# The first 128 tokens of x for three head groups by VectorE's 32x32 turning and a trip through DRAM, in place of TensorE's transposes

## The chip, the core and the metric

The kernel runs on one core of one Trainium2 chip. The metric is the device time of one execution in microseconds (us). A core has five engines that each work through a list of instructions of their own, in order: TensorE (PE, the matrix products; its weight loads are shown as PEld), VectorE (DVE), ScalarE (ACT), GpSimd (POOL) and SyncE (SP). DMA transfers are issued by SP, ACT or POOL and carried out by 16 DMA engines. SBUF is the memory on the core, 128 partitions wide; PSUM is the small memory into which TensorE writes.

## The reference, cut to what matters

One inference step of a one-layer decoder with a gated MLP half and a state-space (SSD) half, for 256 prompt tokens and 8 samples of 8 tokens. What the change touches is the SSD half:

```python
xbc, new_conv = causal_depthwise_conv(xbc, conv_state, conv_w, conv_b)
xbc = jax.nn.silu(xbc)
xs = xbc[..., :SSM_WIDTH].reshape(bsz, L, SSM_HEADS, SSM_HEAD_DIM).astype(f32)   # 32 heads of 64
dt = jax.nn.softplus(dt_raw.astype(f32) + dt_bias.astype(f32))
...
xdt = (x * dt[..., None]).reshape(bsz, nc, q, G, R, P)          # 4 groups of 8 heads, chunks of 128 tokens
cb = jnp.einsum("bctgn,bcsgn->bctsg", cc, bc)
y_diag = jnp.einsum("bctsgr,bcsgrp->bctgrp", cb[..., None] * decay, xdt)
states = jnp.einsum("bcsgn,bcsgr,bcsgrp->bcgrpn", bc, decay_states, xdt)
```

The product `xdt` is needed with tokens on the partitions, since both `y_diag` and `states` sum over tokens; the convolution that makes `xs` leaves channels on the partitions. So x has to be turned. The prompt is two chunks of 128 tokens (c = 0 and c = 1); the 64 sample tokens are a third piece.

## The kernel before

All 320 tokens stand side by side in the free dimension and channels on the partitions. The large products go through `project` (columns of `w_in` and `ffn_w_up`) and `chunk_out` (rows of `w_out` and `ffn_w_down`). Each loads weights slab by slab (`slab`, line 109: 512 KB on SP's queue into three buffers in turn, a rounded copy `whi` made by ACT on line 123, the remainder `wlo` by DVE on line 124) and runs three products per block on TensorE (lines 134 to 136).

The SSD half works through four groups of 8 heads, each a generator `ssd(g)` (line 901). Its steps are put between the large products: after every slab `tick` (line 157) advances the first task in the list when enough products have gone by (`yield 24, 0` means 24 products later). Four generators stand one behind the other. The x of group g + 1 is made by `heads_in_next(g + 1)` (line 1209) while group g is under way: `conv_proj` projects, convolves, and its last activation (lines 459 and 460, on ACT) writes block j of `xs`.

At the beginning of a group (lines 959 to 965), for each chunk c, TensorE turns four blocks of 128 channels by 128 tokens of `xs` with `by_token` (line 410) into a PSUM tile `xt_ps`, and `times` (line 923) multiplies it with `dt` into `xdt[:, c]` on DVE. From chunk 0 POOL makes the decayed copy `x0d` (`decayed(0, 0)`, line 930), ACT and DVE split it into `x0s` (lines 981 and 982, a tile with the tag `xsp`), and 48 products later TensorE multiplies it with B into `s_ps` (line 991). Then come the steps n = 0 to 12 (line 1106), 24 products apart. At steps 2, 5, 7 and 10 `end(i)` updates two sample states each (products `up_ps`, line 1018, which read the tile `xsp` of the samples); at steps 6 and 12 `products` makes y (`y_ps`, line 1086); at step 11 `mask_c` prepares the next group's C mask on DVE. `tc.issue_after(lowered[0])` puts DVE instructions behind the last `wlo` that the code has issued at that point. The tag `xsp` has one buffer: `x0s`, then `xsp`, then the next group's `x0s` take it in turn, each after the last reader of the one before.

A way to turn by DVE and DRAM is there already for B: `to_tokens` (line 414) turns 32x32 blocks of 64 tokens on DVE into a tile with the tag `pv` (four buffers), and POOL writes them to `b_d` in DRAM with four DMAs per 64 tokens; they are loaded again with tokens on partitions (`b_raw`, line 839). Within a row the channels then stand as (i j f), i the 32-row block, j the block of 128, f within 32, and `in_order` (line 423) reads them in their order.

The build derives the waits between engines from the tiles that instructions read and write, and lays out each engine's list from the order in the code, priorities (`first()`, `tc.high_priority`), the `issue_after` edges, and when it estimates operands to be ready; so instructions of one engine need not run in the order of the code.

Of the kernel before, what the change touches and what calls it, by code (L numbers as in the profile page):

```python
# [8 lines left out]
F32 = mybir.dt.float32  # L9
# [3 lines left out]
ALU = mybir.AluOpType  # L13
# [3 lines left out]
P = 128  # L17
NP = 256
NB, TS = 8, 8
NS = NB * TS  # L20
NT = NP + NS
# [12 lines left out]
def hybrid_step(  # L34
# [10 lines left out]
    act, dve, pool, pe, sp = nc.scalar, nc.vector, nc.gpsimd, nc.tensor, nc.sync  # L45
# [4 lines left out]
    dr = ctx.enter_context(tc.tile_pool(name="dr", bufs=1, space=DRAM))  # L50
    wp = ctx.enter_context(tc.tile_pool(name="wp", bufs=3))
    tp = ctx.enter_context(tc.tile_pool(name="tp", bufs=2))
# [3 lines left out]
    def misc(name):  # L56
        return ms.tile([P, 512], F32, tag="ms", name=name)
# [6 lines left out]
    with tc.high_priority(offset=300000):  # L64
        dve.memset(ones, 1.0)

        ps = misc("early")
# [39 lines left out]
    slab_load, split_after, both, rounded, lowered = [], [None], [], [], []  # L107
# [248 lines left out]
    tot_d = dr.tile([NH, NB], F32, name="tot_d")  # L356
    s1_d, x1_d = ([dr.tile([P, 512], F32, name=f"{n}_d{g}") for g in range(3)] for n in ("s1", "x1"))
    b_d = dr.tile([NT, 512], F32, name="b_d")
    v_d = [dr.tile([NT, 2 * P], F32, name=f"v_d{i}") for i in range(KD // 2)]
    ssq_d = [dr.tile([P, NT // 32], F32, name=f"ssq_d{i}") for i in range(4)]  # L360

# [48 lines left out]
    def by_token(ps, x, c):  # L410

        pe.transpose(ps, x[:, P * c:P * c + P], ident)  # L412

    def to_tokens(x, rows):

        for o in range(0, NT, NS):
            t = tp.tile([P, NT], F32, tag="pv", name="turned", bufs=4)[:, :4 * NS].rearrange("p (r f) -> p r f", r=2)
            dve.transpose(out=t.rearrange("p r (j f) -> p r j f", j=4), in_=x[:, :, o:o + NS].rearrange("p j (r t) -> p r j t", t=32))
            for i in range(4):
                pool.dma_start(rows[o:o + NS, P * i:P * i + P].rearrange("(r t) f -> t r f", t=32), t[32 * i:32 * i + 32])  # L420
            yield

    def in_order(ap):
# [3 lines left out]
    with ExitStack() as mctx:  # L427
        op = mctx.enter_context(tc.tile_pool(name="op", bufs=1))
# [42 lines left out]
        dt = op.tile([P, 5, NH], F32, name="dt")  # L471
# [115 lines left out]
        with tc.tile_pool(name="gp", bufs=1) as gp:  # L587
# [42 lines left out]
            def root():  # L630

                dve.tensor_tensor(out=acc[:, 0, :], in0=acc[:, 0, :], in1=acc[:, 1, :], op=ALU.add)
                ps = misc("tsum")
                for c in range(2):
                    pe.matmul(ps[:, c:c + 1], acc[:, 0, P * c:P * c + P], ones[:, 0:1], start=True, stop=True)
                for h in range(2):
                    pe.matmul(ps[64 * h:64 * h + 64, 2:3], acc[:, 0, NP:NT], ones[:, 0:1], start=True, stop=True, tile_position=(0, 64 * h))
                return rsqrt_of(ps[:, 0:3], 1.0 / D, 3)
# [42 lines left out]
            ps = [mm.tile([P, 512], F32, tag="mm", name=f"ps_v{j}") for j in range(4)] + [misc(f"ps_v{j}") for j in (4, 5)]  # L681
            for kt in range(KD):
                x_ready(kt, 1)
                x = [h[:, kt, :] for h in hT]
# [24 lines left out]
                if kt == 15:  # L709
                    r = root()  # L710
# [6 lines left out]
            turned = [gp.tile([P, 4, NT], F32, tag="vf", name="turned", bufs=2).rearrange("p j n -> p (j n)") for _ in range(2)]  # L717
            turned = [t[:, 2 * NT * h:2 * NT * h + 2 * NT].rearrange("p (s j f) -> p s j f", j=2, f=32) for t in turned for h in range(2)]
# [121 lines left out]
            for g in range(4):  # L840
# [3 lines left out]
                if g < 3:  # L844
                    uf = gate_up(g + 1)
                    if g == 2:
                        b4 = [[tp.tile([P, NT], F32, tag="pv", name="b4", bufs=4)[:, :256] for _ in range(2)] for _ in range(2)]
                        for i in range(2):
                            o = NP + 32 * i
# [8 lines left out]
        with tc.tile_pool(name="sd", bufs=1) as sd:  # L858
# [36 lines left out]
            def by_head(ap):  # L895
                return ap.rearrange("p (h d) -> p h d", d=64)

            x_of = {0: x0}
            rest, y_made, b_later = [], {}, []

            def ssd(g):

                xs = x_of[g]
                h0 = 8 * g
# [17 lines left out]
                xdt = sd.tile([P, 3, 512], F32, tag="xdt", name="xdt", bufs=1)  # L922
                def times(out, ps, c, at=slice(0, P), h=slice(0, 8)):
                    n = h.stop - h.start
                    dve.tensor_tensor(out=by_head(out), in0=by_head(ps),
                                      in1=dt[at, c, h0 + h.start:h0 + h.stop].unsqueeze(2).to_broadcast([at.stop - at.start, n, 64]), op=ALU.mult)

                def decayed(i, c):
                    xde = sd.tile([P, 512], F32, tag="xde", name="xde", bufs=2)
                    pool.tensor_tensor(out=by_head(xde), in0=by_head(xdt[:, c, :]),  # L930
                                       in1=dec[:, i, h0:h0 + 8].unsqueeze(2).to_broadcast([P, 8, 64]), op=ALU.mult)
                    return xde
# [20 lines left out]
                def samples_rows(ps):  # L953
                    for r in range(2):
                        at, hs = slice(NS - NS * r, P - NS * r), slice(256 * r, 256 * r + 256)
                        dve.tensor_tensor(out=by_head(xdt[at, 2, hs]), in0=by_head(ps[:NS, hs]),
                                          in1=dt[:NS, 2, h0 + 4 * r:h0 + 4 * r + 4].unsqueeze(2).to_broadcast([NS, 4, 64]), op=ALU.mult)

                for c in range(2):
                    ps = misc("xt_ps")  # L960
                    for j in range(4):
                        by_token(ps[:, P * j:P * j + P], xs[:, j], c)
                    times(xdt[:, c, :], ps, c)
                    if c == 0:
                        x0d = decayed(0, 0)
                ps = misc("cb_ps")
# [3 lines left out]
                for r in range(2):  # L970
# [3 lines left out]
                                  in0=ps[:, :NP].rearrange("p (c t) -> p c t", c=2),  # L974
                                  in1=upper.unsqueeze(1).to_broadcast([P, 2, P]), op=ALU.mult)
# [51 lines left out]
                def yo_to_xdt():  # L1027

                    for r in range(2):
                        at = slice(64 * r, 64 * r + 64)  # L1030
                        dve.tensor_tensor(out=by_head(xdt[at, 2, 256 * r:256 * r + 256]), in0=by_head(ps_yo[at, :256]),
                                          in1=ed[at, g, :].unsqueeze(2).to_broadcast([64, 4, 64]), op=ALU.mult)
# [10 lines left out]
                xsp = sd.tile([P, 2, 512], F32R, tag="xsp", name="xsp", bufs=1)  # L1043
# [62 lines left out]
                for n in range(13 - e):  # L1106
                    if n == 0:
                        samples_rows(ps_x)
                        yo_to_xdt()
                    if n in ends and not (n == 10 and g == 3):  # L1110
                        end(ends[n])
                    for i in picks.get(n, ()):
                        bms[i] = picked(i)
                    if n in (6, 12 - e):
                        products(0 if n == 6 else 2)
                        products(1 if n == 6 else 3)
                    with tc.issue_after(last_made[0]):
                        for j in decays_of.get(n, ()):
                            cs_of[j] = load_sums(j)
                        if n == 8 and g < 3:  # L1120
                            first_sums[g + 1] = load_sums(0, g + 1, h0 + 8)
                        if n in states and states[n][0] < 4:
                            sts_of[states[n][0]].append(load_state(*states[n]))
                    if n == 9 and g == 3:
                        b_raw = sd.tile([P, 512], F32, tag="st", name="b_later", bufs=6)
                        sp.dma_start(b_raw, b_d[P:2 * P])
                        b_later.append(b_raw)
                    if n == 11 and g < 3:
                        with tc.issue_after(lowered[0]):
                            mask_c(g + 1)  # L1130
                    if n in shrinks:
                        shrunk(shrinks[n], sts[shrinks[n]])
                    if n in heads:
                        with tc.issue_after(last_made[0]):
                            decays(heads[n])
                    if n < 12 - e:
                        yield 24, 48 if n + 1 in (0, 1, 2, 5, 7, 10) and (g < 3 or n < 7) else 0
# [3 lines left out]
                                   in1=dec[:, 2, h0:h0 + 8].unsqueeze(2).to_broadcast([P, 8, 64]), op=ALU.mult)  # L1141
# [98 lines left out]
            with first():  # L1240
# [4 lines left out]
                with tc.issue_after(sums_ins[-1]):  # L1245
                    ps = token_sums(*one)
# [3 lines left out]
                r = rsqrt_by_root(most, ps, 1.0 / D)  # L1250
# [54 lines left out]
    with tc.tile_pool(name="fp", bufs=1) as fp:  # L1305
# [118 lines left out]
        ps = misc("tsum")  # L1424
# [7 lines left out]
        v, s, r, t = (fp.tile([P, SN], F32, name=f"last_{i}") for i in "vsrt")  # L1432
# [7 lines left out]
        f, x = (t.rearrange("p s k f -> p s (k f)") for t in (f_tok, x1_tok))  # L1440
# [121 lines left out]
```

## Time and profile before

| | |
|---|---|
| median of 3 runs | 1748.12 us (1747.77 to 1748.39) |
| the profiled execution | 1747.88 us |
| its span, first to last instruction | 1746.1 us |
| granted TensorE clock | 0.999 |
| DMA moved | 303.85 MB, mean 174 GB/s |
| first and last turning of prompt x on TensorE | 419.2 and 670.0 us |

The span is the time between the first and the last instruction in the trace; what the profiled execution took beyond it (1.8 us) lies around it. In a row of the timeline the columns are start, length, engine, line, operation, output and inputs; in square brackets stands idle time of the engine before it and who ended it. The chain of waits is followed back from the last instruction, at each step to what released it or to the instruction before it on its engine; its pieces don't overlap, whereas TensorE's own records do, since products are pipelined. "Landing" is the time from the issue of a DMA to its end.

### The profile page before, as it was taken

Reading aid. Unit: us, or ns where it says so; the run is one execution under the profiler, and the core shown is the slowest. Engines: PE = TensorE matmul, PEld = TensorE weight load, DVE = VectorE, ACT = ScalarE, POOL = GpSimd, SP = SyncE. Lnnn points to the kernel's source line nnn. Section 1 sums busy time; section 2 is a strip of 40 time slices with the busy share of each in tenths; the row PEclk is TensorE's granted clock in tenths of the full one; section 3 lists DMA queues with packets and bytes.
Section 4 is the critical chain, followed back from the end, with each engine's and each line's share of the span. In section 5 each row is a group of like instructions: output and inputs, shape, how many; then the busy total and the mean of one; then the engine's idle time right before and its main releaser. Section 6 shows DMA issues by size and latency. Waiting matters only on the chain.

```text
span 1746.1 us, 31126 instructions
## 1 busy us (share of the span) xinstructions
PE 1738.4 (100%) x12063; PEld 1719.7 (98%) x12063; DVE 1177.1 (67%) x2009; ACT 819.9 (47%) x1198; POOL 324.9 (19%) x684
## 2 busy tenths in 40 slices
PE   9999999999999999999999999999999999999998
PEld 9999999999999999999999999999999999999997
DVE  6549863667978787778854566565756565657587
ACT  6344545334656664646544434343434343343336
POOL 2432230000423323121210101020201010101002
PEclk9999999999999999999999999999999999999999
DMA  8776665455676776655654454545444545454543
GB/s 259 227 233 182 183 176 157 153 165 186 208 228 205 220 231 209 211 184 160 189 157 148 153 153 148 153 152 147 159 145 152 154 149 153 151 154 150 148 157 109
DMA packets 228803, 303.85 MB, mean 174 GB/s; under 512 B 21680, under 2 KB 152624, under 8 KB 228464
## 3 DMA queue, kind: packets, MB, share of 16 engines
q1 hardware_dynamic: 211264, 272.68, 51.4%
q0 software_dynamic: 6176, 13.87, 2.7%
q10 hardware_dynamic: 11216, 15.31, 2.5%
q8 instruction: 95, 1.56, 0.4%
q14 instruction: 52, 0.43, 0.1%
HBM read 280.80 MB, written 19.69 MB: 172 GB/s over the span
## 4 chain that ended last, share of the span: by engine, by line
PE 99%; ACT 0%; DVE 0%; issue 0%; ACTq 0%
PE ps L134 21%; PE ps L135 20%; PE ps L136 20%; PE pd L134 10%; PE pd L136 10%; PE pd L135 10%; PE y_ps L1086 1%; PE ps_v L134 1%; PE ps_v L136 1%; PE ps_v L135 1%; PE yo_ps L1001 0%; PE up_ps L1018 0%; PE sg L808 0%; PE early L69 0%; PE xt_ps L412 0%; PE s_ps L991 0%
## 5 line engine op out<-in xcount | busy, mean ns | idle before, releaser
L124 DVE TENSOR_TENSOR wlo<-wraw,whi 128x1024 fp32r<-128x1024 f32 (+2 forms) x480 | 583.8, 1217 | 422.2 <-ACT whi L123 419.7
L123 ACT CAST whi<-wraw 128x1024 fp32r<-128x1024 f32 (+2 forms) x479 | 495.4, 1034 | 694.0 <-PE ps L135 388.2
L134 PE MATMUL ps<-h_hi,whi 128*128 128x320 f32 x2428 | 752.3, 310 | 0.0
L135 PE MATMUL ps<-h_lo,whi 128*128 128x320 f32 x2428 | 750.7, 309 | 0.0
L136 PE MATMUL ps<-h_hi,wlo 128*128 128x320 f32 x2428 | 750.1, 309 | 0.0
L134 PEld LDWEIGHTS ps<-h_hi,whi 128*128 128x128 f32 x2428 | 455.6, 188 | 3.1 <-issue 1.3
L135 PEld LDWEIGHTS ps<-h_lo,whi 128*128 128x128 f32 x2428 | 455.8, 188 | 0.4
L136 PEld LDWEIGHTS ps<-h_hi,wlo 128*128 128x128 f32 x2428 | 455.6, 188 | 0.0
L134 PE MATMUL pd<-fhi,whi 128*128 128x320 f32 x704 | 217.4, 309 | 0.0
L135 PE MATMUL pd<-flo,whi 128*128 128x320 f32 x704 | 217.4, 309 | 0.0
L136 PE MATMUL pd<-fhi,wlo 128*128 128x320 f32 x704 | 217.4, 309 | 0.0
L134 PE MATMUL pd<-ohi,whi 128*128 128x320 f32 x448 | 138.7, 310 | 0.0
L136 PE MATMUL pd<-ohi,wlo 128*128 128x320 f32 x448 | 138.3, 309 | 0.0
L135 PE MATMUL pd<-olo,whi 128*128 128x320 f32 x448 | 138.3, 309 | 0.0
L1341 POOL COPY ptf<-pad 128x2 f32<-128x2 f32 x88 | 22.0, 250 | 602.4 <-DVE pad L1329 601.7
L136 PEld LDWEIGHTS pd<-fhi,wlo 128*128 128x128 f32 x704 | 132.4, 188 | 0.0
L134 PEld LDWEIGHTS pd<-fhi,whi 128*128 128x128 f32 x704 | 132.3, 188 | 0.0
L135 PEld LDWEIGHTS pd<-flo,whi 128*128 128x128 f32 x704 | 132.3, 188 | 0.0
L247 DVE TENSOR_TENSOR acc_ffn<-acc_ffn,pd 128x320 f32<-128x320 f32 (+1 forms) x161 | 77.1, 480 | 29.9 <-PE pd L136 28.3
L134 PEld LDWEIGHTS pd<-ohi,whi 128*128 128x128 f32 x448 | 84.1, 188 | 0.6
L135 PEld LDWEIGHTS pd<-olo,whi 128*128 128x128 f32 x448 | 84.1, 188 | 0.3
L136 PEld LDWEIGHTS pd<-ohi,wlo 128*128 128x128 f32 x448 | 84.1, 188 | 0.0
(353 smaller groups left out, 1726.3 us busy)
## 6 DMA issues: line engine op xcount, KB each, us to landing
wraw<-in_ffn_w_up SPq DMA_DIRECT2D x176, 512.0 KB, 3.7
wraw<-in_w_in SPq DMA_DIRECT2D x132, 512.0 KB, 3.9
wraw<-in_ffn_w_down SPq DMA_DIRECT2D x88, 512.0 KB, 3.4
wraw<-in_w_out SPq DMA_DIRECT2D x64, 512.0 KB, 3.5
st<-in_state_ssm SPq DMA_DIRECT2D x40, 256.0 KB, 4.3
out_ssm_state_sample<-st ACTq DMA_DIRECT2D x30, 256.0 KB, 2.5
cs<-dacs_d SPq DMA_DIRECT2D x16, 320.0 KB, 5.4
wraw<-in_w_in SPq DMA_DIRECT2D x12, 384.0 KB, 4.4
```

Source lines behind the costliest of these rows:

```text
L123: rounded[:] = [act.copy(hi, raw).ins]
L124: lowered[:] = [dve.tensor_tensor(out=lo, in0=raw, in1=hi.bitcast(F32), op=ALU.subtract).ins]
L134: pe.matmul(ps, whi, xhi, start=first, stop=False)
L135: pe.matmul(ps, whi, xlo, start=False, stop=False)
L136: last_made[0] = pe.matmul(ps, wlo, xhi, start=False, stop=last).ins
L247: added_last[:] = [dve.tensor_tensor(out=acc[:, nb, ts], in0=acc[:, nb, ts], in1=ps[:, ts], op=ALU.add).ins]
L1086: pe.matmul(ps[64 * i:64 * i + 64, cols], w(hl), x(hl, m, cpx), tile_position=(0, 64 * i), **flags)
L1341: pool.tensor_copy(ptf[:, k, :], pad[:, 256:258])
```

## The change

In groups 1 to 3 (the 2nd to 4th), chunk 0 of x no longer goes through TensorE.

- A new helper `tokens_at` turns 64 tokens on DVE and writes them with two DMAs on POOL's queue (one per 32 tokens, all four 32-row blocks at once, 128 partitions). `to_tokens`, and so B, uses it too: B's 20 writes become 10.
- At step 8 of group g, `tokens_at` turns and writes tokens 0 to 127 of the next group's x (two calls, four writes of 64 KB) to a new DRAM tensor `x_d`, the DVE part behind the last `wlo`.
- At step 11 POOL loads them, 256 KB with tokens on partitions, into a tile with the tag `xsp`.
- At the beginning of the next group `times_raw` multiplies that tile with `dt` in two DVE instructions (one per half of the channel blocks, which also put channels in their order), where `times` read four turned blocks from PSUM.
- Chunk 1, the samples and the first group stay as they were.

```diff
+    x_d = [dr.tile([P, 512], F32, name=f"x_d{g}") for g in range(1, 4)]
...
+    def tokens_at(x, rows, o):
+
+        t = tp.tile([P, NT], F32, tag="pv", name="turned", bufs=4)[:, :4 * NS].rearrange("p (r f) -> p r f", r=2)
+        dve.transpose(out=t.rearrange("p r (j f) -> p r j f", j=4), in_=x[:, :, o:o + NS].rearrange("p j (r t) -> p r j t", t=32))
+        for r in range(2):
+            pool.dma_start(rows[o + 32 * r:o + 32 * r + 32].rearrange("t (i f) -> i t f", i=4), t[:, r])
+
     def to_tokens(x, rows):
 
         for o in range(0, NT, NS):
-            t = tp.tile([P, NT], F32, tag="pv", name="turned", bufs=4)[:, :4 * NS].rearrange("p (r f) -> p r f", r=2)
-            dve.transpose(out=t.rearrange("p r (j f) -> p r j f", j=4), in_=x[:, :, o:o + NS].rearrange("p j (r t) -> p r j t", t=32))
-            for i in range(4):
-                pool.dma_start(rows[o:o + NS, P * i:P * i + P].rearrange("(r t) f -> t r f", t=32), t[32 * i:32 * i + 32])
+            tokens_at(x, rows, o)
             yield
...
-            rest, y_made, b_later = [], {}, []
+            rest, y_made, b_later, raw_of = [], {}, [], {}
...
+                def times_raw(out, raw, c):
+
+                    for h in range(2):
+                        dve.tensor_tensor(out=out.rearrange("p (j h i f) -> p h j i f", j=4, h=2, f=32)[:, h],
+                                          in0=raw[:, 256 * h:256 * h + 256].rearrange("p (i j f) -> p j i f", j=4, f=32),
+                                          in1=dt[:, c, h0:h0 + 8].rearrange("p (j h) -> p h j", h=2)[:, h]
+                                              .unsqueeze(2).unsqueeze(3).to_broadcast([P, 4, 2, 32]), op=ALU.mult)
...
                 for c in range(2):
-                    ps = misc("xt_ps")
-                    for j in range(4):
-                        by_token(ps[:, P * j:P * j + P], xs[:, j], c)
-                    times(xdt[:, c, :], ps, c)
+                    if c == 0 and g:
+                        times_raw(xdt[:, c, :], raw_of[g], c)
+                    else:
+                        ps = misc("xt_ps")
+                        for j in range(4):
+                            by_token(ps[:, P * j:P * j + P], xs[:, j], c)
+                        times(xdt[:, c, :], ps, c)
                     if c == 0:
                         x0d = decayed(0, 0)
...
+                    if n == 8 and g < 3:
+                        with tc.issue_after(lowered[0]):
+                            for o in range(2):
+                                tokens_at(x_of[g + 1], x_d[g], NS * o)
                     if n == 11 and g < 3:
+                        raw_of[g + 1] = sd.tile([P, 2, 512], F32, tag="xsp", name="x_raw", bufs=1)[:, 0]
+                        pool.dma_start(raw_of[g + 1], x_d[g])
                         with tc.issue_after(lowered[0]):
                             mask_c(g + 1)
```

## The prediction, written before the changed kernel was run

> **What bounds the kernel now.** I read the page's busy times and chain first, then what TensorE (PE) waited for, then the chain piece by piece around the four groups.
>
> ```profile
> PE 1738.4 (100%) x12063; PEld 1719.7 (98%) x12063; DVE 1177.1 (67%) x2009; ACT 819.9 (47%) x1198; POOL 324.9 (19%) x684
> ...
> PE 99%; ACT 0%; DVE 0%; issue 0%; ACTq 0%
> ```
>
> The chain that ended last is PE from one end to the other. The list of PE's waits agrees: it has two rows in the whole span, one at the start and one at the very end.
>
> ```profile
> PE early L69 <- DVE ones L65: 1.1, 1, 1.1
> PE both L1454 <- ACT f_tok L1452: 1.0, 1, 1.0
> ```
>
> So there is no stall that the change could cure. It can only gain what it takes off PE's own list, and it loses whatever makes PE wait for the first time. The pieces of the chain (start, length, what) that bear on it:
>
> ```profile
> 491.06 0.47 PE up_ps L1018 x2
> 503.98 0.87 PE xt_ps L412 x8
> 516.34 0.69 PE s_ps L991 x3
> 572.08 0.47 PE up_ps L1018 x2
> 585.00 0.87 PE xt_ps L412 x8
> 593.84 0.69 PE s_ps L991 x3
> 669.54 0.87 PE xt_ps L412 x8
> 678.38 0.69 PE s_ps L991 x3
> ```
>
> For the 2nd to 4th group these give PE's eight turnings of x (four for tokens 0 to 127, four for 128 to 255) and the point at which PE asks for the product of turned x, decay and B (`s_ps`, whose operand `x0s` comes from the first 128 tokens). In the two earlier groups the `up_ps` piece is the last reader of `xsp`, whose place the new tile takes.
>
> **What is removed.** Eight turnings fill 0.87 us of the chain, 0.109 us each. Four fall away in each of three groups: 12 x 0.109 = 1.31 us. That is the whole possible gain by these rows, 0.07% of the time. A turning's own record is longer:
>
> ```profile
> L412 PE MATMUL xt_ps<-ident,xs x32: 270/272/273, 419.3 to 670.1; 128*128 128x128 f32 x32
> ```
>
> but that counts its passage through the pipeline, beside its neighbours; the chain's pitch is what the next instruction feels, so I take 0.109 and keep 0.272 as the upper end (3.26 us for 12).
>
> **What is added, and its prices.** Each of the three trips has two VectorE (DVE) turnings of 128x256, four writes issued by GpSimd (POOL), one 256 KB load issued by POOL, and two DVE multiplications of 128x256 in place of one of 128x512 from PSUM. The token turning of B, which exists already, shows the first kinds:
>
> ```profile
> L418 DVE STREAM_TRANSPOSE turned<-bT x5: 402/432/446, 238.5 to 245.0; 128x256 f32<-128x256 f32 x5
> ```
> ```profile
> L420 POOL DMA_DIRECT2D b_d<-turned x20: 539/539/591, 239.2 to 249.4; - x20
> ...
> DMA to landing us min/median/max: 1.8/2.9/3.9
> ```
> ```profile
> L839 POOL DMA_DIRECT2D b_raw<-b_d x2: 554/560/566, 249.9 to 251.1; - x2
> ...
> DMA to landing us min/median/max: 4.0/5.1/6.2
> ```
>
> The load's exact twin is `b_raw`: 4.0 to 6.2 us from issue to landing, 5.1 taken. As outer ends I use other 256 KB loads of POOL (norm parameters), 3.8 and 7.1:
>
> ```profile
> L760 POOL DMA_DIRECT2D lg<-in_gate_ln_g x4: 537/552/566, 58.2 to 164.2; - x4
> ...
> DMA to landing us min/median/max: 3.8/4.5/7.1
> ```
>
> A new write has 64 KB where the old had 32. The page's issues put 80 KB at a median of 3.6:
>
> ```profile
> v_d<-turned POOLq DMA_DIRECT2D x32, 80.0 KB, 3.6
> ```
>
> I estimate 3.3 us for 64 KB, between 2.9 and 3.6, with 1.8 and 3.9 as ends. The multiplication of 128x256 is taken at 0.41 us, from a row below.
>
> Engine time is covered. Per group DVE gets 2 x 0.43 + 2 x 0.41 - 0.69 = 1.0 us more, POOL 5 x 0.55 = 2.8 us more. B's own writes go from 20 to 10, so POOL sheds some 5 us there; B's turned rows are first used in the first group, which begins at 419.3 us, 168 us after the last load of them is issued (251.1), so this is worth nothing at the end. If the DVE cover were gone (no idle time at all), the three groups would cost 3.0 us; DVE is at 67%.
>
> **Is the trip back in time?** It can begin when the last block of the next group's x is written (L459 on ScalarE, ACT), the load when `xsp` is free and the writes have landed. For the 2nd group `xsp` frees at 491.06 + 0.47 = 491.5, the load lands at 496.6, and what follows it (4.85 us, worked out next) ends at 501.5, 14.9 us before its `s_ps`. For the 3rd: 572.55, 577.7, 582.5, 11 us before. The x of both groups is complete, and its writes issued, before `xsp` frees.
>
> ```profile
> 667.65 0.73 POOL L1063 TENSOR_TENSOR cpx<-cpx,cT 128x256 f32<-128x256 f32 x1
> ```
>
> While POOL waits for `xsp` (up to some 7 us in the 2nd group) its queue stands. What can stand behind is a decay multiplication of L1063, whose reader is a product (`y_ps`) later in its group, and the two at a group's end, which nothing on PE reads soon; I cost that at nothing, since POOL is 19% busy and each of them has a lead over its reader. Without the lead each would cost its 0.73 us at least.
>
> The 4th group is the tight one, because its x is complete only 7.7 us before PE's turnings (661.86 against 669.54), so that x is what the trip waits for:
>
> ```profile
> 661.45 0.41 ACT L459 ACTIVATE xs<-cv 128x256 f32<-128x256 f32 x1
> ...
> 674.75 1.05 ACT L123 CAST whi<-wraw 128x1024 fp32r<-128x1024 f32 x1 [1.36 <-DVE x0s L982]
> ```
> ```profile
> 661.58 1.23 DVE L124 TENSOR_TENSOR wlo<-wraw,whi 128x1024 fp32r<-128x1024 f32 x1
> ...
> 670.01 0.69 DVE L925 TENSOR_TENSOR xdt<-xt_ps,dt 128x512 f32<-128x512 f32 x1
> ...
> 672.36 0.41 DVE L973 TENSOR_TENSOR cb_cms<-cb_ps,upper 128x256 f32<-128x256 f32 x1
> ...
> 674.06 0.67 DVE L982 TENSOR_TENSOR x0s<-xde,x0s 128x512 fp32r<-128x512 f32 x1
> ```
>
> Step by step. x is complete at 661.9, DVE is in a weight split until 662.8, the two turnings end at 663.2 and 663.7. POOL issues four writes one after the other from 663.2 and starts the last at 664.8. It lands 3.3 later, at 668.1. The load lands 5.1 after that, at 673.2. The two multiplications end at 674.0. From the end of the old multiplication (670.70) to the end of L982 (674.73), by way of L930 and L981, it was 4.03 us; so `x0s` is ready at 678.05. PE now asks for it 0.44 earlier than before (four turnings gone), at 677.94. **The margin is -0.1 us**: the trip takes almost exactly the time there is.
>
> On DVE the multiplication waits for the load, and behind it stand additions into `acc` and a weight split; on ACT the cast of 674.75 stands behind L981. They are late by 2 to 4 us. Their cover is the three weight buffers in turn: when a slab is cast, PE has two others in hand. I cost them at nothing; without that cover PE would wait the same 2 to 4 us. A split that falls in front of the new multiplication delays it by up to 1.23 us. Giving that a chance of about a third, I put the wait at `s_ps` at 0.5 us. Its ends: none (writes 1.8, load 3.8), and writes 3.9, load 7.1, one split in front, which makes 0.1 + 0.6 + 2.0 + 1.23 = 3.9 us.
>
> **Sum:** -1.31 + 0.5 = -0.8 us. The profiled execution took 1747.88 for its span of 1746.1, so it would be 1747.1; that execution lies 0.24 under the median of 1748.12, so the median becomes **1747.3 us**.
>
> By the Trainium skill, DMA: Bandwidth & Descriptors, section on the anatomy of one DMA, a transfer on this path takes about 2.0 us and its bytes over 436,000 per us. That gives estimates of 2.15 us for a write and 2.6 us for the load, 3.65 less than the 8.4 taken, and no wait at all; the 32 KB writes here took 2.9 us, though, where that rule says 2.1, and the loads 5.1, so I stay with the rows.
>
> **The rivals.** *The trip is hidden altogether*: it needs only 0.6 us less somewhere, and L930, within the 4.03, is a step of very uneven length.
>
> ```profile
> L930 POOL TENSOR_TENSOR xde<-xdt,dec x8: 1045/1622/2026, 423.8 to 688.4; 128x512 f32<-128x512 f32 x8
> ```
>
> Then the gain stays whole: 1748.12 - 1.31 = 1746.8 us.
>
> *The 4th group's trip comes late.* PE waits at `s_ps`, in its own order, with everything behind it. It decides from a wait of 1.31 us on, that is `x0s` later than 679.25. The load at 7.1 and a split in front make 0.1 + 2.0 + 1.23 = 3.3 us, net +2.0: 1750.1 us. For it: the margin is nil and all steps are in series. Against it: it happens in one group alone.
>
> *POOL's issues are drawn out by DVE*, and the trip is later still. POOL's rows do show such stretching, the same copy once and again:
>
> ```profile
> 553.29 1.53 POOL L445 COPY pad<-sst 128x24 f32<-128x24 f32 x1
> ...
> 559.41 0.21 POOL L445 COPY pad<-sst 128x24 f32<-128x24 f32 x1
> ```
>
> At 1.32 us more for each of five issues the wait is 0.1 + 6.6 = 6.7 us, net +5.4: 1753.5 us. Against it stand the 20 issues of L420 at 539 to 591 ns beside a busy DVE. The Trainium skill, SBUF — State Buffer, has this as the "DVE blocks DMA" trap: the descriptors of a DMA from this queue cannot be written while DVE holds both ports; the 539 to 591 ns do not show it.
>
> *A turning costs PE its full 0.272 us*: -3.26 us, 1744.9. Against it the chain's 0.87 for eight.
>
> *The change doesn't shift the end*: the build lays out each engine's order anew, and the 0.44 us per group are lost again to another order around `cb_ps`: 1748.1 us. That the turnings stay cannot be; the branch drops them.
>
> **Chances.** Forecast (wait of 0 to 1.3 us at `s_ps`) 0.40; hidden altogether 0.25; late trip 0.22; POOL drawn out 0.07; 0.272 us each 0.03; no shift 0.03. The range 1746.5 to 1750.5 holds the first two, no shift and most of the late trip. A measurement of this kernel can tell about 0.2% (3.5 us) from no change: faster than 1744.6 needs more than the whole chain price, 0.03; slower than 1751.6 is the drawn-out case with the tail of the late trip, 0.11; within, 0.86.
>
> **What would show it.** PE's instructions fall by 12, and the `xt_ps` pieces of the 2nd to 4th group are 0.44 long. PE's waits have a new row `s_ps` on x0s, once, in the 4th group, under 1.3 us. The load lands 4 to 6 us after its issue and the writes 2 to 4. The 2nd and 3rd groups' loads land near 497 and 578, less the time saved ahead. Wrong would be: a wait in the 2nd or 3rd group; a wait of PE for `wlo` or for a freed bank; issues on POOL over 0.7 us; a gain over 1.5 us with no wait gone.

## The result and the profile after

The changed kernel takes 1753.81 us (median of 8 runs, 1750.98 to 1755.5) where the kernel before takes 1748.31 on the same chip (8 runs, 1747.67 to 1748.78): a ratio of 1.0031, 95% interval 1.0021 to 1.0042. It is slower by 5.5 us; 1747.3 had been forecast. The profiled execution took 1753.69 us for a span of 1751.8, where before's took 1747.88.

The page of the changed kernel, engines first (busy time, share, instructions), then the shares of the chain that ended last:

```profile
PE 1740.8 (99%) x12051; PEld 1720.4 (98%) x12051; DVE 1177.4 (67%) x2018; ACT 819.6 (47%) x1198; POOL 324.5 (19%) x689
...
PE 95%; DVE 2%; ACT 1%; issue 1%; DMA 0%; POOL 0%; ACTq 0%; POOLq 0%; DVEq 0%
```

PE has the 12 instructions less that were to go, and yet it is busy 2.4 us longer, and the chain now passes through other engines. The list of PE's waits (total, times, longest) says where:

```profile
PE ps L134 <- DVE acc_mix L247: 2.9, 2, 2.3
PE early L69 <- DVE ones L65: 1.1, 1, 1.1
PE both L1476 <- ACT f_tok L1474: 1.0, 1, 1.0
PE ps L136 <- DVE wlo L124: 0.4, 1, 0.4
```

The first row is new, and it isn't the wait at `s_ps` that was forecast. PE's own timeline shows that both waits lie in the 4th group:

```profile
675.10 0.31 PE L135 MATMUL ps<-h_lo,whi 128*128 128x320 f32 x1
675.24 0.31 PE L136 MATMUL ps<-h_hi,wlo 128*128 128x320 f32 x1
677.88 0.63 PE L134 MATMUL ps<-h_hi,whi 128*128 128x320 f32 x1 [2.33 <-DVE acc_mix L247]
...
680.38 0.63 PE L134 MATMUL ps<-h_hi,whi 128*128 128x320 f32 x1 [0.54 <-DVE acc_mix L247]
...
681.08 0.47 PE L136 MATMUL ps<-h_hi,wlo 128*128 128x320 f32 x1
681.35 0.47 PE L134 MATMUL ps<-h_hi,whi 128*128 128x320 f32 x1
```

`ps` is a PSUM bank of `project`, which begins its next stretch of `w_in` here (`heads_out(2)`, four banks side by side). `pd` and `ps` share the four banks of the tag `mm`. The third bank still holds block 14 of the product that `chunk_out` has just made, the fourth block 15, until DVE has added them into `acc` (L247). DVE's timeline at that place:

```profile
662.61 0.77 DVE L418 STREAM_TRANSPOSE turned<-xs 128x256 f32<-128x256 f32 x2
...
670.01 1.22 DVE L124 TENSOR_TENSOR wlo<-wraw,whi 128x1024 fp32r<-128x1024 f32 x1
676.67 0.76 DVE L936 TENSOR_TENSOR xdt<-x_raw,dt 128x256 f32<-128x256 f32 x2 [5.44 <-DMA x_raw<-x_d]
677.35 0.48 DVE L247 TENSOR_TENSOR acc_mix<-acc_mix,pd 128x320 f32<-128x320 f32 x1
...
679.24 0.69 DVE L998 TENSOR_TENSOR x0s<-xde,x0s 128x512 fp32r<-128x512 f32 x1 [0.19 <-ACT x0s L997]
679.85 0.48 DVE L247 TENSOR_TENSOR acc_mix<-acc_mix,pd 128x320 f32<-128x320 f32 x1
```

DVE reached the new multiplication (L936) at 671.2 and stood for 5.44 us until the load had landed, with the two additions behind it. Each of them releases one of PE's two waits. So the stall runs from the DMA through DVE's order to a PSUM bank.

The trip itself, from POOL's timeline and from the instructions of the write (L420; count, shortest, median and longest duration in ns, first and last start) in this window:

```profile
664.45 2.77 POOL L420 DMA_DIRECT2D x_d<-turned  x4 [18.57 <-DVE cb_cms L887]
...
672.56 0.62 POOL L1150 DMA_DIRECT2D x_raw<-x_d  x1 [3.57 <-DMA x_d<-turned]
```
```profile
L420 POOL DMA_DIRECT2D x_d<-turned x4: 689/696/716, 664.5 to 666.5; - x4
...
DMA to landing us min/median/max: 3.6/4.0/5.2
```

Nearly every link is longer than forecast: the first write starts at 664.45 (forecast 663.2), issues take 0.69 us (0.54), the last write lands 5.2 us after its start (3.3). Only the load is shorter: it starts at 672.56, and L936 at 676.67, 4.1 us later (5.1).

There is a second loss behind the first. The view by stretches gives, after the length, the busy time of PE, its weight loads, DVE, ACT and POOL, then the clock that was granted, the share of the DMA engines and GB/s:

```profile
676.00:678.00 2.00, 0.12 (x1) 0.12 (x1) 1.33 (x4) 0.00 (x0) 0.48 (x1) 0.88 0.00 0
678.00:680.00 2.00, 1.85 (x6) 1.44 (x6) 1.77 (x6) 1.42 (x2) 0.55 (x1) 0.50 0.00 0
680.00:682.00 2.00, 1.62 (x6) 1.62 (x7) 1.86 (x3) 0.15 (x1) 0.00 (x0) 0.50 0.00 0
```

Behind the first hole PE works at half the clock: in its timeline above, two products at 681 start 0.27 us apart, two ahead of the hole 0.14. That is why PE is *busier* in a kernel in which it does less. This fall doesn't come in every execution: seven of the eight show a mean granted clock of 0.997 or 0.998, the eighth 0.999, as before has. The eighth is the fastest, 1750.98 us, and still 2.7 us slower than before.

The chain's pieces show the earlier groups and the place where the loss arises:

```profile
419.75 0.87 PE xt_ps L413 x8
504.28 0.43 PE xt_ps L413 x4
516.18 0.70 PE s_ps L1007 x3
584.84 0.44 PE xt_ps L413 x4
593.22 0.70 PE s_ps L1007 x3
682.35 1.28 PE s_ps L1007 x3
800.82 0.46 PE up_ps L1034 x2
```

For comparison, the first and the last of these in the chain of before, whose other pieces stand in the prediction:

```profile
419.46 0.87 PE xt_ps L412 x8
795.85 0.46 PE up_ps L1018 x2
```

I use the distance from the first turning to the last `up_ps` as a ruler for the four groups, because it leaves out what varies ahead of them: the first turning lies between 419.1 and 420.1 us in the kernels of this study. Before it is 376.39 us, after 381.07: 4.68 more. Up to `s_ps` of the 2nd group PE is ahead by 0.45 us (96.88 before, 96.43 after), up to that of the 3rd by 0.91, and up to that of the 4th it is *behind* by 3.68 (258.92 before, 262.60 after). Of the remaining 1.1 us of the 5.8 between the profiled executions, 0.3 is the later first turning and 0.7 the hand-over to the large products behind the groups, where the 0.4 us wait for `wlo` lies.

### The profile page after: what moved, and what is told of

Its sections match the earlier page's. It is cut to its first block, busy times and chain, and to the rows that moved or that the text cites. A ratio compares the mean times of both kernels' runs of the same rounds, so it can differ in the third digit from the quotient of the medians.

```text
span 1751.8 us, 31136 instructions
## 1 busy us (share of the span) xinstructions
PE 1740.8 (99%) x12051; PEld 1720.4 (98%) x12051; DVE 1177.4 (67%) x2018; ACT 819.6 (47%) x1198; POOL 324.5 (19%) x689
## 4 chain that ended last, share of the span: by engine, by line
PE 95%; DVE 2%; ACT 1%; issue 1%; DMA 0%; POOL 0%; ACTq 0%; POOLq 0%; DVEq 0%
PE ps L134 20%; PE ps L136 20%; PE ps L135 20%; PE pd L134 10%; PE pd L135 10%; PE pd L136 10%; PE ps_v L136 1%; PE ps_v L135 1%; PE ps_v L134 1%; PE y_ps L1102 1%; DVE wlo L124 1%; DVE acc_mix L1299 0%; PE yo_ps L1017 0%; PE sg L813 0%; PE up_ps L1034 0%
## 5 line engine op out<-in xcount | busy, mean ns | idle before, releaser
L124 DVE TENSOR_TENSOR wlo<-wraw,whi 128x1024 fp32r<-128x1024 f32 (+2 forms) x480 | 582.7, 1215 | 419.1 <-ACT whi L123 416.2
L247 DVE TENSOR_TENSOR acc_ffn<-acc_ffn,pd 128x320 f32<-128x320 f32 (+1 forms) x161 | 77.2, 480 | 29.8 <-PE pd L136 28.2
```

What stands on the lines that cost most here:

```text
L124: lowered[:] = [dve.tensor_tensor(out=lo, in0=raw, in1=hi.bitcast(F32), op=ALU.subtract).ins]
L247: added_last[:] = [dve.tensor_tensor(out=acc[:, nb, ts], in0=acc[:, nb, ts], in1=ps[:, ts], op=ALU.add).ins]
```

## The experiments

Two theories stood against each other at first. Theory A: the 4th group alone costs time, because DVE waits there for a load that goes through its own writes, with additions into `acc` behind it; the other two groups gain 0.109 us per turning. The rivals: some part of the trip costs time in every group (POOL's queue, DVE's additional work, B's new writes), or the late x0s itself stops PE. In the table, "groups" is the ruler's difference to before in one profiled execution; the ratio is to before on the same chip, whose median was 1748.31, 1748.19 for the next four, 1748.05 for the four behind them, and 1748.39 for the last. The medians are of 8 to 11 runs, that of the multiplications on POOL of 4. That kernel's chain doesn't pass through the first turning; its ruler begins 0.16 us behind the turning's own record (419.16), which is the distance in the kernel before and in the changed one.

| kernel | median us | ratio, 95% interval | groups, us |
|---|---|---|---|
| the change | 1753.81 | 1.0031 (1.0021 to 1.0042) | +4.68 |
| trip in the 2nd and 3rd group only | 1747.31 | 0.9995 (0.9987 to 1.0004) | -0.90 |
| trip in the 4th group only | 1751.07 | 1.0015 (1.0006 to 1.0024) | +2.19 |
| 4th group's load without its writes | 1747.54 | 0.9997 (0.9988 to 1.0006) | -1.37 |
| 4th group's multiplications on POOL | 1754.21 | 1.0035 (1.0022 to 1.0049) | +5.32 |
| 4th group's multiplications later | 1748.20 | 1.0001 (0.9993 to 1.001) | -0.88 |
| PE kept at work in its holes | 1752.15 | 1.0025 (1.0014 to 1.0035) | +2.95 |
| B's new writes only | 1748.47 | 1.0002 (0.9993 to 1.0011) | 0.00 |
| later, and both chunks in the 2nd and 3rd | 1747.55 | 0.9998 (0.9989 to 1.0007) | -2.22 |
| both chunks in the 2nd and 3rd, none in the 4th | 1747.47 | 0.9994 (0.9985 to 1.0003) | -1.77 |

**The trip in the 2nd and 3rd group only.** The 4th group goes back to TensorE.

```diff
-                    if c == 0 and g:
+                    if c == 0 and 0 < g < 3:
...
-                    if n == 8 and g < 3:
+                    if n == 8 and g < 2:
...
+                        if g < 2:
```

> The 4th group turns its first 128 tokens on TensorE again; the trip stays in the 2nd and 3rd group, and B's writes stay as changed. Theory A (the loss comes from the 4th group alone, where VectorE stands 5.4 us in front of the late load and the additions behind it hold PSUM banks): all loss gone and two groups' gain left, 8 x 0.109 = 0.87 us, so about 0.9 us under the kernel before (ratio 0.9995), no wait of TensorE on acc. Theory B (the added instructions and DMAs cost by themselves, in every group): two thirds of the loss stay, about 3.7 us over the kernel before.

Measured: 0.88 us under before in the medians, 0.90 on the ruler, which is eight turnings of 0.109 (0.87). PE's list of waits is that of before:

```profile
PE early L69 <- DVE ones L65: 1.1, 1, 1.1
PE both L1477 <- ACT f_tok L1475: 1.0, 1, 1.0
```

So the trip costs PE nothing where it has time; the whole loss belongs to the 4th group. The interval of the ratio reaches over 1, so the gain itself rests on the ruler.

**The trip in the 4th group only.** The opposite.

```diff
-                    if c == 0 and g:
+                    if c == 0 and g == 3:
...
-                    if n == 8 and g < 3:
+                    if n == 8 and g == 2:
...
+                        if g == 2:
```

> The trip is made in the 4th group alone; the 2nd and 3rd turn on TensorE. Theory A: the whole loss and a third of the gain, about 0.9 us over the changed kernel, 6.4 us over the kernel before, with TensorE waiting some 3 us on additions into acc and a granted clock of 0.5 for some 6 us after it. Theory B: a third of the loss, about 1.8 us over the kernel before.

Measured: slower by 2.9 us, less than half of what was expected. The place is right, PE waits for the same two additions, but less long, and the clock stays up. PE's timeline, DVE's and one stretch:

```profile
676.66 0.41 PE L134 MATMUL ps<-h_hi,whi 128*128 128x320 f32 x1 [0.75 <-DVE acc_mix L247]
...
679.16 0.41 PE L134 MATMUL ps<-h_hi,whi 128*128 128x320 f32 x1 [1.36 <-DVE acc_mix L247]
```
```profile
675.44 0.76 DVE L936 TENSOR_TENSOR xdt<-x_raw,dt 128x256 f32<-128x256 f32 x2 [3.86 <-DMA x_raw<-x_d]
```
```profile
676.00:678.00 2.00, 1.15 (x6) 0.88 (x6) 1.78 (x6) 0.64 (x2) 1.03 (x1) 1.00 0.00 1
```

DVE stood 3.86 us instead of 5.44. Behind the first turning (419.20 here, 419.75 in the changed kernel) POOL's first write starts at the same distance, 244.6 and 244.7 us, but PE still has eight turnings more ahead of the 4th group, so against PE's list the trip begins about 1 us earlier, and it is 0.6 shorter from there to L936 (11.63 us against 12.22). DVE's turnings did move with the gain of the earlier groups: behind the first turning they begin at 242.86 us in the changed kernel and at 243.88 here. What stayed behind in the changed kernel is POOL's first write, so there the gain of the earlier groups made the 4th tighter. The runs of this kernel spread over 4.9 us and those of the changed kernel over 4.5, while 27 of the kernel before spread over 2.3: the size of the loss varies from execution to execution. Here that isn't the clock, as all ten executions show 0.999 or 1.000. On the ruler +2.19 plus the four turnings of 0.44 is 2.63, which is the two holes of 2.11 and 0.26 us more for each: the list counts a hole that much short, since a record reaches 0.16 us past the start of the next product and the first product behind a hole takes 0.41 instead of 0.31.

**The 4th group's load without its writes.** The 4th group loads the rows written for the 3rd, which are long there, so its y and states for the prompt come from the 3rd group's x. All instructions and transfers stay; their order doesn't quite.

```diff
-                        pool.dma_start(raw_of[g + 1], x_d[g])
+                        pool.dma_start(raw_of[g + 1], x_d[min(g, 1)])
```

> As the changed kernel, but the 4th group loads the rows that the 3rd group's x left in DRAM, which were written long before, so its load need not wait for its own writes (group 4's prompt states and y are computed from the wrong x; all instructions, writes and sizes stay). Theory A: the load lands before VectorE reaches the multiplication, TensorE waits nowhere and the clock stays at 1.0: about 1.3 us under the kernel before (ratio 0.9993). Theory B: still some 5.5 us over it. If only part of the wait goes, the lateness of x itself is not the cause.

Measured: -1.37 us on the ruler, where all 12 turnings are 1.31; no wait of PE for a bank. With the same DVE and POOL work and the same number of transfers the loss is gone as soon as the load doesn't follow the group's own writes, which is strong evidence for theory A. But the build also laid out the lists anew: POOL issues the load at 656.74, ahead of the writes, and the multiplication stands on DVE ahead of the additions of blocks 12 to 15.

```profile
666.51 2.00 DVE L936 TENSOR_TENSOR xdt<-x_raw,dt 128x256 f32<-128x256 f32 x2
```

So the run doesn't tell the early load from the earlier place. The median is only 0.65 us under before and its interval holds both 1 and the whole gain.

**The 4th group's multiplications on POOL.** If DVE's wait is the evil, another engine could take it.

```diff
-                        dve.tensor_tensor(out=out.rearrange("p (j h i f) -> p h j i f", j=4, h=2, f=32)[:, h],
+                        (pool if g == 3 else dve).tensor_tensor(out=out.rearrange("p (j h i f) -> p h j i f", j=4, h=2, f=32)[:, h],
```

> As the changed kernel, but in the 4th group GpSimd makes the two multiplications by dt. If VectorE's multiplication as such (A, narrow) is what blocks, its queue is free from 671 to 680 us and the loss falls to the wait at s_ps, at most 3 us over the kernel before. If any VectorE instruction that needs the late rows blocks as well (A, wide): the remainder of x0s (L998) now stands in VectorE's queue in front of the last addition into acc, later by GpSimd's slower multiplications, so TensorE waits about 5 us there and the loss stays at 5 to 8 us.

Measured: no better than the change. DVE no longer stands at the multiplication, but at the next instruction that hangs on it, the remainder of `x0s`, with an addition behind that; PE now waits once, for 5.1 us by its list of waits. It got through eighteen products of `project` first, three blocks, since here the addition of block 14 had gone ahead and only that of block 15 was held up.

```profile
681.06 0.64 PE L134 MATMUL ps<-h_hi,whi 128*128 128x320 f32 x1 [5.06 <-DVE acc_mix L247]
```
```profile
679.11 0.69 DVE L998 TENSOR_TENSOR x0s<-xde,x0s 128x512 fp32r<-128x512 f32 x1 [6.87 <-ACT x0s L997]
...
680.53 0.48 DVE L247 TENSOR_TENSOR acc_mix<-acc_mix,pd 128x320 f32<-128x320 f32 x1
```

So moving one instruction isn't enough: every DVE instruction that depends on the load and has an addition behind it holds a bank.

**The 4th group's multiplications later.** That is done here: chunk 0 of the 4th group comes 24 products later, and behind the last addition that the code has issued by then.

```diff
-                for c in range(2):
+                for c in range(g // 3, 2):
...
+                if g == 3:
+                    yield 24, 0
+                    with tc.issue_after(added_last[0]):
+                        times_raw(xdt[:, 0, :], raw_of[g], 0)
+                    x0d = decayed(0, 0)
```

> As the changed kernel, but in the 4th group the two multiplications, x0d and x0s come 24 products later, the multiplications behind VectorE's last addition into acc of the product under way; s_ps follows 48 products behind them as before. Theory A (VectorE's queue standing at the late load is the whole loss): no addition stands behind the load, TensorE waits nowhere, the clock stays at 1.0, and the gain of all three groups is left, 12 x 0.109 = 1.3 us under the kernel before (ratio 0.9993). Rival (a trip that ends after 677 us is too late for the group in any order): TensorE waits at s_ps or at the products y, 1 us or more over the kernel before.

Measured: the loss is gone, the gain isn't there. DVE still waits 2.02 us for the load, now with the additions ahead of it:

```profile
673.73 0.49 DVE L247 TENSOR_TENSOR acc_mix<-acc_mix,pd 128x320 f32<-128x320 f32 x1 [0.35 <-PE pd L136]
...
676.24 0.76 DVE L936 TENSOR_TENSOR xdt<-x_raw,dt 128x256 f32<-128x256 f32 x2 [2.02 <-DMA x_raw<-x_d]
```

PE waits for no bank and not at `s_ps`, and the clock is 1.00 from 674 to 684. At the `up_ps` piece of 709.02 (710.19 before) the ruler still has the whole gain, 1.36 us. The 0.48 that is lost by 795 is one wait, 0.2 us by the list and 0.26 more as above, in PE's timeline:

```profile
768.19 0.42 PE L135 MATMUL pd<-h_lo,whi 128*128 128x320 f32 x1 [0.17 <-DVE h_lo L401]
```

So the loss lay in the work behind the waiting instruction, in the late operand, or in both. The run doesn't separate these two, since `s_ps` also comes 24 products later.

**PE kept at work in its holes.** How much of the loss is the clock? Sixteen products of ones into a bank of their own fill PE's list ahead of the third and the fourth block of `heads_out(2)`.

```diff
+            warm_ps = misc("warm") if warm and k0 == 0 else None
...
+                if warm_ps is not None and c >= 2:
+                    with tc.issue_after(last_made[0]):
+                        for _ in range(10 if c == 2 else 6):
+                            pe.matmul(warm_ps[:, :P], ones, ones, start=True, stop=True)
...
-                project(w_in, Z0 + 512 * g, z_evac)
+                project(w_in, Z0 + 512 * g, z_evac, warm=g == 2)
```

> The changed kernel with 16 idle products of ones on TensorE, 10 and 6 of them where it waited 2.33 and 0.54 us for PSUM banks (their result is not used). Theory: the wait itself makes the granted clock fall to 0.5, and 6.7 us at half speed cost some 3.2 us beside the 2.9 us of waiting. With TensorE busy the clock stays at 1.0 and the time falls to some 2 to 3 us over the kernel before. Rival: the clock falls for another reason, or the waits alone make the loss: no faster than the changed kernel.

Measured: 1.73 us less than the change on the ruler (4.68 - 2.95). In the medians, each against before on its own chip, it is 1.4 us (5.5 - 4.1), and the intervals of the two ratios overlap. The holes are filled, each of the 16 appearing as two records, and the clock holds:

```profile
675.76 2.39 PE L194 MATMUL warm<-ones 128*128 128x128 f32 x20
678.34 0.42 PE L134 MATMUL ps<-h_hi,whi 128*128 128x320 f32 x1 [0.18 <-DVE acc_mix L252]
679.35 1.50 PE L194 MATMUL warm<-ones 128*128 128x128 f32 x12
```
```profile
678.00:680.00 2.00, 1.82 (x14) 1.66 (x13) 1.75 (x6) 0.95 (x2) 1.02 (x1) 1.00 0.00 0
```

So the half clock is worth 1.7 us of the loss, by one profiled execution of each kernel; more had been expected. At full clock PE gets through the third block sooner and then stands longer in front of the fourth: 1.50 us filled here, where the changed kernel shows 0.54 us idle. What is left, 2.95 + 1.31 = 4.3 us, is the two holes themselves: 2.6 and 1.5 us from the end of one block to the start of the next, and 0.1 us more for the first product behind each.

**B's new writes only.** Without any trip of x; ten writes for B where there were twenty.

```diff
-                    if c == 0 and g:
+                    if False:
...
-                    if n == 8 and g < 3:
+                    if n == 8 and False:
```

> Only the new writing of B's turned rows (10 DMAs of 128 partitions in place of 20 of 32); x is turned on TensorE in all groups as before. Theory A: no change, within 0.3 us of the kernel before. Rival (the new form of writing, 0.69 us per issue and later landing, costs by itself): over 0.5 us slower.

Measured: 0.00 on the ruler; the medians differ by 0.4 us and the interval holds 1. B's writes have no part in it.

**Later, and both chunks in the 2nd and 3rd group.** The version with the later multiplications, and twice the trip where there is time: 20 turnings gone.

```diff
-                            for o in range(2):
+                            for o in range(4 if g < 2 else 2):
...
+                        raw_of[g + 1] = sd.tile([P, 2, 512], F32, tag="xsp", name="x_raw", bufs=1)
+                        for c in range(2 if g < 2 else 1):
+                            pool.dma_start(raw_of[g + 1][:, c], x_d[g][P * c:P * c + P])
```

> As later_last, and in the 2nd and 3rd group both chunks of 128 tokens make the trip (eight writes, two loads, four multiplications). Theory A: 20 turnings are gone, 20 x 0.109 = 2.2 us under the kernel before (ratio 0.9988), TensorE waits nowhere. Rival (twice the trips is too much for GpSimd's queue or comes late in the 2nd or 3rd group): a wait of TensorE on acc, s_ps or up_ps there, and less gain than later_last.

Measured: the ruler gives -2.22, 20 times 0.109 being 2.18, and the profiled execution took 1746.23. The median is 0.5 us under before, with runs from 1746.23 to 1749.44. The profile has one new wait, 0.2 us, for `wlo`. Why the other runs took more than the profiled one isn't known.

**Both chunks in the 2nd and 3rd group, none in the 4th.** The same without the tight group: 16 turnings gone.

> The 2nd and 3rd group take both chunks of x by VectorE and the trip, the 4th group has both on TensorE again. By the theory of the run with the trip in the 2nd and 3rd group alone (each turning on TensorE costs 0.109 us, and no trip of these two groups is late), 16 turnings leave: 16 x 0.109 = 1.75 us under the kernel before, ratio 0.9990, and no wait of PE beside the two of before. A rival: with two trips in a group POOL issues twice the writes and VectorE turns twice as much, so the second trip lands late or holds VectorE in front of additions into acc; then PE shows waits for acc_mix in the 2nd or 3rd group and the time is at or above that of the run with one chunk (0.9 under before).

Measured: -1.77 on the ruler (16 times 0.109 is 1.74), and no wait of PE beside the two of before. Twice as many writes at once do land later, the load waits for them, and there is still room:

```profile
L420 POOL DMA_DIRECT2D x_d<-turned x16: 687/689/735, 475.5 to 568.0; - x16
...
  POOL x_raw L1152: 6.2, 2
...
DMA to landing us min/median/max: 4.9/6.6/8.1
```

The median is 0.9 us under before and not 1.75; the interval holds both, and 1 as well. In this profiled execution the first turning came at 419.94, 0.48 later than in that of before, the part behind the groups was 0.2 longer and that outside the span another 0.2, so of 1.77 on the ruler 0.87 is left in the time. No version here beats the kernel before by more than a measurement can tell. What the ruler shows is that 0.109 us per turning is to be had, as far as the trip has time.

## Why the prediction was wrong

**What held.** The bound (PE's own list, no stall to cure) and the price of a turning, 0.109 us: 8, 12, 16 and 20 turnings gave 0.90, 1.37, 1.77 and 2.22 us on the ruler. The 0.272 us of its own record would have given 2.2 to 5.4. The 2nd and the 3rd group: the pieces `xt_ps` are 0.43 and 0.44 long, the loads were issued at 492.1 and 572.7 (forecast 491.5 and 572.55), and PE waited for nothing. The slack was smaller than forecast, though: `x0s` was ready 10.1 and 6.6 us before its `s_ps`, not 14.9 and 11. The loads landed at 496.0 and 577.9, but on DVE the multiplications stood behind other work until 502.47 and 582.46, and one of them took up to 1.26 us where 0.41 had been taken. B's writes are worth nothing at the end.

**The step that failed** is the sentence on what stands behind the waiting multiplication: additions into `acc` and a weight split, covered by "the three weight buffers in turn", and costed at nothing. The prediction priced what the weight split releases, weights, and not what the additions release: banks. `chunk_out` and `project` share four banks, each emptied by one addition. At the change from the one to the other PE has work for as many blocks as there are empty banks: it began `project` at 673.63, and after twelve products, 1.8 us later, it stood. The order that did it can be seen before the change. There, too, the addition of block 15 stands on DVE behind the remainder of `x0s` (L982, at 674.06), on DVE's timeline of before:

```profile
675.06 0.47 DVE L247 TENSOR_TENSOR acc_mix<-acc_mix,pd 128x320 f32<-128x320 f32 x1
```

It ended at 675.53, and PE, which began `project` at 674.70, came to that bank at 677.34. That slack of 1.8 us is what the prediction left out. It gave a price for the case without cover, "PE would wait the same 2 to 4 us", and named a wait for a freed bank as what would refute it. (Two smaller signs that it named came as well: a wait for `wlo`, 0.4 us, and issues on POOL of over 0.7 us, up to 0.717.) The waits came to 2.9 us in the list, about 4.3 us with the clock held up.

**The length of the trip** was mis-sized, each link by its own amount. Until the last write starts it took 1.7 us more (666.5 against 664.8): 1.25 because POOL's first write started 1.1 us behind the end of *both* turnings (663.38), and 0.45 through three issues at 0.69 us instead of 0.54. The last write took 1.9 us more to land, some 0.8 us passed between that and the issue of the load, and the load took 1.0 less. Together the multiplication could begin 3.5 us later than forecast, at 676.67. `x0s` was ready at 679.93 instead of 678.05, only 1.9 us later, since the way to it from the multiplication took 2.5 us and not 4.03. That gave the additions more to wait for, but the forecast's own times would not have avoided the wait. With `x0s` at 678.05 PE would have had block 15's bank at about 678.5 (0.45 later, as here) and would have come to it at 676.3, eighteen products behind 673.63: an estimate of 2.2 us from these rows. And in the run with the 4th group only, where DVE stood 3.86 us, PE still waited 2.1.

The late start has a releaser that I hadn't looked for. The changed kernel's first write was released, by the profile, not by the second turning (ended 663.38) but by a later DVE instruction (L887, a small product for the next group's C mask); with the trip in the 4th group only it was released by the turning. No run varied that alone.

**The rival "late trip"** had the right group and the wrong place. `s_ps` would have been due at 677.36 (258.92 less 1.31 behind the first turning), and `x0s` came 2.6 us after that, so PE would have waited at `s_ps` had it not stood for the banks. The two lie over each other, and with both gone, by an early load or by a later place, the loss is gone. What each would have cost alone wasn't tried.

**What the prediction didn't have at all** is the clock. 1.7 us of the loss, by the run with PE kept at work, arises after PE has its bank, because the hole cost it half its clock for a while. It explains why a loss of 4.3 us became 6 on the ruler (4.68 and the 1.31 that had been gained).

**Open** are the 0.7 us in the hand-over behind the groups, which appear in the changed kernel, in the version with later multiplications, and mostly in the one with both chunks as well, each time beside a wait for `wlo` of 0.2 to 0.4 us, and the late `h_lo` of the version with later multiplications. No run explains either.

## What to carry to other kernels

When an instruction on an in-order engine gets a new wait, list every instruction behind it and what each one releases; those that empty PSUM banks leave the tensor engine only as many blocks of time as it has empty banks, which here was 1.8 us. Count the slack of a trip through DRAM from the moment at which its data is complete, and not from its place in the code: where what it made was ready 6.6 us and more ahead of its use it cost nothing, and nothing when doubled, and where there was no slack it took back several times what it had saved. And where the tensor engine does all the work, price a new hole with the clock that may fall behind it.

## What the runs showed of the hardware

**The half clock lasted 3.41 us, or twice that.** The clock at its two edges, first in the changed kernel, then in the one with the multiplications on POOL (the column behind POOL's):

```profile
677.50:677.60 0.10, 0.00 (x0) 0.00 (x0) 0.10 (x1) 0.00 (x0) 0.08 (x1) 0.57 0.00 0
684.30:684.40 0.10, 0.10 (x1) 0.00 (x0) 0.10 (x1) 0.00 (x0) 0.00 (x0) 0.79 0.54 205
```
```profile
680.60:680.70 0.10, 0.00 (x0) 0.00 (x0) 0.10 (x2) 0.00 (x0) 0.00 (x0) 0.60 0.00 0
684.00:684.10 0.10, 0.10 (x2) 0.02 (x1) 0.10 (x1) 0.00 (x0) 0.00 (x0) 0.83 0.78 246
```

With 1.00 before and 0.50 behind each fall, the shares put the edges at 677.51 and 684.34, and at 680.62 and 684.03: half clock for 6.83 us in the one and 3.41 in the other. One execution of each shows this; it fits a clock that is decided in stretches of 3.41 us. The Trainium skill, TensorE: Matmul & The Clock Gate, Part 1, says that the clock is halved after an idle window of about 3.4 us and restored after a busy one; the length of the window agrees. That the whole window must be idle, as one may read it, does not: in the changed kernel PE worked until about 675.5, so of the 3.41 us before the fall it was at work for some 1.4. In the other run it stopped at about 675.9 and kept its clock until 680.62, 4.7 us later. In the 3.41 us behind the fall PE was busy for 2.50 in the changed kernel, and the clock stayed halved; in the other run it was busy for 2.97, and the clock came back. A hole of 2.3 us thus halved the clock where some 2 us of it lay in one such stretch, and the holes of 0.75 and 1.36 us in the run with the 4th group only did not.

**A write with 512 B rows on all 128 partitions takes POOL 0.69 us to issue**, in every kernel that has it, beside a busy DVE or an idle one; the narrower one of the kernel before took 0.54. Its 64 KB landed 2.7 to 7.3 us after the issue in the changed kernel, up to 8.1 with eight in a row. The Trainium skill, DMA: Bandwidth & Descriptors, section on the anatomy of one DMA, gives 2.0 us and the bytes over 436,000 per us, an estimate of 2.15: the fastest here took 2.7.
